# Weight sums by VectorE instead of accumulating DMAs, and w_down loaded one chunk earlier, in a streaming encoder trunk

## The chip, the core and the metric

The kernel runs on one NeuronCore of a Trainium2 chip. The core has a matrix engine (TensorE, PE in the profile), a vector engine (VectorE, DVE), a scalar engine (ScalarE, ACT), GpSimd (POOL) and SyncE (SP), which here only issues DMAs. Every engine works through its own queue in order, and waits at the head of it for the semaphores of what it reads and overwrites. The metric is the device time of one execution in microseconds; the median of several runs is compared.

## The reference

Two layers of an encoder trunk run on 512 prompt frames and 64 sample frames (576 tokens) of width 1024. Each layer has a mixer with three kinds of attention and then a gated feed-forward, which is where the change lies:

```python
x = x + merge_branches(o_a, o_b, o_c, gate_pre, b_gate[l], w_branch[l], w_out[l])
xn = rmsnorm(x, norm_ffn[l])
gu = xn @ w_up                      # (tokens, 1024) @ (1024, 2 * 2816)
g, u = gu[..., :D_FF], gu[..., D_FF:]
c = conv_b + sum_k conv_w[k] * shifted(g, k)     # causal, width 3
h = gelu(c) * u
x = x + h @ w_down                  # (tokens, 2816) @ (2816, 1024)
```

All inputs, weights and outputs are float32.

## The kernel before

The 2816 hidden columns are 22 blocks f of 128. A float32 product is made of three matmuls on rounded operands: every operand is split into a high part (a cast) and a low part (the operand minus its high part), and high times high, high times low and low times high are summed in PSUM. The 576 tokens are two halves of 288, so a matmul has 288 columns.

Blocks 0 to 3 (`ffn_f`) compute gate and up columns directly. Blocks 4 to 21 (`unit_f`) use a Strassen-Winograd scheme on the two-by-two product of (gate, up) columns, each cut into an upper and a lower half of the 1024 rows, with the two token halves. It takes seven products per block instead of eight: A11, P, R, A12, Q, A22, V, in this order, of 4 row tiles times 3 matmuls, so 84 matmuls. The weight operands of the seven are, with G and U for gate and up columns and 1, 2 for upper and lower rows: A11 = G1, A12 = G2, A22 = U2, P = U1 + U2, R = U1 + G1, Q = P + G1, V = Q + G2.

`wforms` prepares the raw operands of every block, one after another. It uses three raw buffers of 512 KB: r1 holds P in its first half and R in its second, r0 holds G1 and G2, and q holds Q and V; a22 (256 KB, U2) is a tile of the general pool of 40 slots. In the kernel before, U1 is loaded twice into r1, once for each half; r0 and a22 are loaded; GpSimd then issues two accumulating DMAs, which add a22 to the first half and G1 to the second; VectorE computes Q and V from them. `wparts` splits a raw operand: ScalarE casts the high part; the low part comes from VectorE, or, for A11, A12 and A22 (`by_dma`), from ScalarE writing minus the high part and GpSimd issuing an accumulating DMA that adds the raw operand (line 1361). `wparts` for a block waits until TensorE has been given the same form of the block before.

The three loads of the next block wait for their buffers: r1 until P and R of this block are split and Q is made, r0 until A11 and A12 are split and R, Q and V are made, a22 until A22 is split.

Between the blocks stand the down products, in chunks of 2 x 128 output columns, one behind each block: with a group of four hidden blocks a chunk has 4 outputs of 12 matmuls, 48 in all (blocks 8 to 20), with a group of two 24 (blocks 4 to 7). Most chunks bring their own weights through `down_own`: two loads of raw w_down (tiles dr), then casts (dh) by ScalarE and low parts (dl) by VectorE. `all_own` runs these one chunk after another.

The order of all queues is written by a planner while the program is built. `charge` advances a clock for each compute engine by an estimated cost; generators (`spawn`, `tick`) emit their next step when the clock of TensorE has come to their own time. `pause(ns)` puts a generator off by so much of the planned TensorE clock, and `until` until a condition on what has been emitted holds. Nothing of this exists at run time: it only fixes where in each queue an instruction stands. Semaphores do the rest. PSUM has five banks of the kind "z"; A11 and A12 share one (ScalarE copies A11 away to `s` before A12 adds to it, line 1473, and copies A12 to `gp` afterwards, lines 1479 and 1481), P and Q share another, and four outputs of a down chunk take one each until VectorE has added them to x. Behind a block, `tail` runs the convolution (`conv_steps`), the GELU product `ge`, and the split of the result into hh and hl.

In the profile's names, wr are the raw weights (r1, r0, q, a22), m0f13A is the product bank of A11 and A12 of block 13 in layer 0, whi...a and wlo...a its weight parts, eh and el the parts of P and R (b) and A22 (d), md a down product. Layer 0 is the 0 behind the first letter, layer 1 the 1.

Of the kernel before, what the change touches and what calls it, by code (L numbers as in the profile page):

```python
# [14 lines left out]
ALU = mybir.AluOpType  # L15

P = 128
D = 1024
# [29 lines left out]
def trunk_kernel(ctx: ExitStack, tc: tile.TileContext, a: dict, o: dict):  # L48
    nc = tc.nc
    dma = nc.sync.dma_start  # L50
# [14 lines left out]
    def slot(nm, dt=F32, w=TOK):  # L65
        return sp_.tile([P, GW], dt, tag="s", name=nm, bufs=NS)[:, 0:w]
# [29 lines left out]
    def charge(eng, cost):  # L96
        start = clk[eng] if cx["eng"] == eng and cx["last"] == cx["t"] else max(clk[eng], cx["t"])
        clk[eng] = start + cost
        cx["t"] = cx["last"] = clk[eng] + 70
        cx["eng"] = eng  # L100
# [39 lines left out]
    vector = Engine(nc.vector, "DVE", dve_cost)  # L140
# [11 lines left out]
    def spawn(label, g, first=False):  # L152
        gens.insert(0 if first else len(gens), [label, g, cx["t"]])
# [30 lines left out]
    def pause(ns):  # L184
        cx["t"] = clk["PE"] + ns
        yield

    def until(cond):
        while not cond():
            cx["t"] = clk["PE"] + 1  # L190
            yield
# [1000 lines left out]
    def layer(l):  # L1192
# [65 lines left out]
        def ffn_f(f):  # L1258
# [27 lines left out]
            def fin():  # L1286
# [8 lines left out]

            chunk(f"g{nm}", a["w_up"][l][:, f * P:(f + 1) * P], ND, act, evg, pre_ev=pre,
                  pre=begin_ffn if f == 0 else (lambda: spawn("wf", wforms())) if f == NORD - 1 else None, norm=[1] if f == 0 else None,
                  post=lambda: (spawn(f"c{l}{f}", conv()), spawn("forms", forms()) if f == 0 else None))

# [56 lines left out]
        def low(out, src, hi, by_dma):  # L1356

            if by_dma:
                scalar.activation(out, hi.bitcast(F32), AF.Copy, scale=-1.0)
                charge("POOL", 900)  # L1360
                nc.gpsimd.dma_start(out, src, accum_op=ALU.add)
            else:
                vector.tensor_tensor(out, src, hi.bitcast(F32), op=ALU.subtract)
# [4 lines left out]
        def half_tile(nm, dt=F32):  # L1368
            return slot(nm, dt)[:, 0:512].rearrange("p (k c) -> p k c", k=4)

        def wparts(f, nm, forms_, src, by_dma, small):

            if f > NORD:
                yield from until(lambda: all((f - 1, n) in used for n in forms_))
            elif nm == "a":
                yield from until(lambda: "last" in fast)
            elif nm in "cd":
                yield from until(lambda: "go" in fast)
            yield
            key = f"{l}{f}{nm}"  # L1380
            if small:
                pairs = [(half_tile(f"eh{key}{j}", F32R), half_tile(f"el{key}{j}", F32R))
                         for j in range(len(forms_))]
            else:
                h_, l_ = (wp.tile([P, 8, P], F32R, tag=t, name=f"{t}{key}", bufs=2) for t in ("whi", "wlo"))
                pairs = [(h_[:, 4 * j:4 * j + 4, :], l_[:, 4 * j:4 * j + 4, :]) for j in range(2)]
            for j, n in enumerate(forms_):
                hi, lo = pairs[j]
                scalar.copy(hi, src[:, 4 * j:4 * j + 4, :])
                yield  # L1390
                low(lo, src[:, 4 * j:4 * j + 4, :], hi, by_dma)
                ws[f, n] = (hi, lo)
                made.add((f, n))
                yield

        def wforms():

            w = a["w_up"][l]
            rr = lambda t: t.rearrange("(k p) c -> p k c", p=P)
            for f in range(NORD, NF):  # L1400
                gc, uc = w[:, f * P:(f + 1) * P], w[:, F + f * P:F + (f + 1) * P]

                def raw(i, *need):
                    if f > NORD:
                        yield from until(lambda: all((f - 1, n) in made for n in need))
                    return wp.tile([P, 8, P], F32, tag="raw", name=f"wr{l}{f}{i}", bufs=3)

                r1 = yield from raw(1, "P", "R")
                for j in range(2):
                    dma(r1[:, 4 * j:4 * j + 4, :], rr(uc[0:D // 2]))  # L1410
                r0 = yield from raw(0, "A11", "A12")
                dma(r0, rr(gc))
                if f > NORD:
                    yield from until(lambda: (f - 1, "A22") in made)
                a22 = half_tile(f"wr{l}{f}3")
                dma(a22, rr(uc[D // 2:D]))
                spawn("wa", wparts(f, "a", ("A11", "A12"), r0, f != NORD + 1, False), True)
                yield from pause(5000)
                for j, t in enumerate((a22, r0[:, 0:4, :])):
                    charge("POOL", 900)  # L1420
                    nc.gpsimd.dma_start(r1[:, 4 * j:4 * j + 4, :], t, accum_op=ALU.add)  # L1421
                spawn("wd", wparts(f, "d", ("A22",), a22, True, True), True)
                yield from pause(4500)
                spawn("wb", wparts(f, "b", ("P", "R"), r1, False, True), True)
                q = yield from raw(2, "Q", "V")
                vector.tensor_tensor(q[:, 0:4, :], r1[:, 0:4, :], r0[:, 0:4, :], op=ALU.add)
                yield
                vector.tensor_tensor(q[:, 4:8, :], q[:, 0:4, :], r0[:, 4:8, :], op=ALU.add)
                yield
                spawn("wc", wparts(f, "c", ("Q", "V"), q, False, False), True)  # L1430

        def down_own(c, fs, d2, after):

            yield from until(after)
            n = len(fs) // 2
            src = down_w(fs, d2).rearrange("(k p) c -> p k c", p=P)
            key = f"{l}{fs[0]}{d2}"
            raw = [slot(f"dr{key}{j}")[:, 0:n * 256].rearrange("p (k c) -> p k c", k=n) for j in range(2)]
            for j in range(2):
                dma(raw[j], src[:, n * j:n * j + n, :])  # L1440
            yield from pause(4000)
            hi, lo = ([slot(f"d{t}{key}{j}", F32R)[:, 0:n * 256].rearrange("p (k c) -> p k c", k=n)
                       for j in range(2)] for t in "hl")
            for j in range(2):
                scalar.copy(hi[j], raw[j])
                yield
                vector.tensor_tensor(lo[j], raw[j], hi[j].bitcast(F32), op=ALU.subtract)
                yield
            c["lo"] = [lo[k // n][:, k % n, :] for k in range(2 * n)]
            c["hi"] = [hi[k // n][:, k % n, :] for k in range(2 * n)]  # L1450
# [108 lines left out]
        def down_w(fs, d2):  # L1559
            return a["w_down"][l][fs[0] * P:(fs[-1] + 1) * P, d2 * 2 * P:(d2 + 1) * 2 * P]  # L1560
# [53 lines left out]
        def all_own():  # L1614
            for n, (c, fs, d2) in enumerate(owns):
                yield from down_own(c, fs, d2, lambda: n == 0 or n - 1 in issued)
# [386 lines left out]
```

## Time and profile before

| | us |
|---|---|
| median of three runs (2237.34 to 2241.85) | 2240.66 |
| the profiled execution | 2234.81 |
| its span, from the first to the last instruction | 2232.7 |
| mean granted TensorE clock over the span | 0.984 |

All durations below come from the profiled execution. The granted clock is 1.00 at 2.4 GHz and 0.5 at 1.2 GHz; a value between is a mean over time. In a row of a timeline, the bracket at the end gives the engine's idle time before the instruction and what ended it. In names of groups, buffer numbers are left out. A busy share of TensorE does not say that it works at its peak, since the ends of pipelined matmuls are modelled; the number of matmuls in a stretch says more.

### The profile page before, as it was taken

What the parts mean: (1) busy time and instruction counts of PE and PEld (TensorE: products, weight loads), DVE (VectorE), ACT (ScalarE), POOL (GpSimd) and SP (SyncE); (2) the same over time, 40 slices, a digit from 0 to 9 for tenths busy, and PEclk for the clock granted to TensorE, in tenths of its full rate; (3) what the DMA queues carried; (4) which work ended last, traced back from release to release, by engine and by line L of the source; (5) the groups of instructions that cost most, each with busy time, mean ns of one, the idle gap of its engine ahead of it and who ended that gap; (6) DMA issues with size and microseconds to landing.
All of it is one profiled execution on the core that took longest, in us unless ns stands there. A gap on an engine that the chain in (4) does not pass through costs nothing.

```text
span 2232.7 us, 40248 instructions
## 1 busy us (share of the span) xinstructions
PE 2128.5 (95%) x15479; PEld 2073.0 (93%) x15479; DVE 1465.1 (66%) x3076; ACT 1230.1 (55%) x2485; POOL 467.4 (21%) x687
## 2 busy tenths in 40 slices
PE   8999999999999899898899999999999999998897
PEld 7999999999999898898899999999999998988897
DVE  7876666776568666455678766677755777646555
ACT  5657776555446555445345677754553455545444
POOL 2111220111213322222110122101103233222221
PEclk9999999999999999999999999999999999999999
DMA  7452222332326887666343222233224277766661
GB/s 214 124 147 71 80 71 77 104 93 78 121 83 134 175 185 155 148 148 142 106 121 103 81 70 72 77 101 100 86 79 124 81 169 167 166 156 140 149 158 58
DMA packets 375657, 263.19 MB, mean 118 GB/s; under 512 B 15600, under 2 KB 344242, under 8 KB 375402
## 3 DMA queue, kind: packets, MB, share of 16 engines
q1 hardware_dynamic: 344906, 204.32, 31.2%
q0 software_dynamic: 30560, 56.31, 14.7%
q8 instruction: 122, 2.00, 0.4%
q14 instruction: 69, 0.57, 0.1%
HBM read 185.98 MB, written 25.83 MB: 95 GB/s over the span
## 4 chain that ended last, share of the span: by engine, by line
PE 71%; DMA 13%; DVE 8%; ACT 3%; issue 3%; POOL 1%; SPq 0%; POOLq 0%; DVEq 0%; ACTq 0%
PE md L146 8%; DMA wr<-in_w_up 6%; PE mo L146 4%; DMA wr<-wr 4%; PE mg1a L146 2%; PE mg0a L146 2%; PE mg1b L146 2%; PE mg0b L146 2%; PE mg1c L146 2%; PE mg0c L146 2%; PE mv1a L146 1%; PE mb1a L146 1%; PE mb0a L146 1%; PE mv1b L146 1%; PE mv0b L146 1%
## 5 line engine op out<-in xcount | busy, mean ns | idle before, releaser
L117 DVE TENSOR_TENSOR wr<-wr,wr 128x512 f32<-128x512 f32 x72 | 49.6, 690 | 185.0 <-DMA wr<-wr 184.2
L1421 POOL DMA_DIRECT2D wr<-wr x72 | 65.2, 1095 | 278.7 <-DMA wr<-in_w_up 274.9
L117 DVE TENSOR_TENSOR x<-md,x 128x288 f32<-128x288 f32 x224 | 97.0, 451 | 33.1 <-PE md L146 32.8
L117 ACT CAST dh<-dr 128x512 fp32r<-128x512 f32 (+1 forms) x72 | 41.5, 577 | 134.4 <-DMA dr<-in_w_down 134.4
L146 PE MATMUL md<-hh1f,dh 128*128 128x288 f32 x256 | 81.6, 319 | 16.0 <-ACT gp1f L117 15.3
L146 PE MATMUL md<-hh0f,dh 128*128 128x288 f32 x256 | 81.4, 318 | 16.1 <-ACT gp0f L117 15.4
L146 PE MATMUL md<-hh1f,dl 128*128 128x288 f32 x256 | 82.4, 322 | 9.6 <-DVE dl L117 8.8
L146 PE MATMUL md<-hh0f,dl 128*128 128x288 f32 x256 | 81.7, 319 | 8.1 <-DVE dl L117 7.7
L146 PE MATMUL md<-hl0f,dh 128*128 128x288 f32 x256 | 80.0, 313 | 0.0
L117 DVE TENSOR_TENSOR dl<-dr,dh 128x512 fp32r<-128x512 f32 (+1 forms) x72 | 45.1, 627 | 53.3 <-ACT dh L117 53.3
L146 PE MATMUL md<-hl1f,dh 128*128 128x288 f32 x256 | 79.8, 312 | 0.0
L146 PE MATMUL mo<-ml,whio 128*128 128x288 f32 x256 | 75.7, 296 | 0.8 <-DVE ml L117 0.8
L146 PE MATMUL mo<-mh,whio 128*128 128x288 f32 x256 | 75.7, 296 | 0.0
L146 PE MATMUL mo<-mh,wloo 128*128 128x288 f32 x256 | 75.5, 295 | 0.0
L146 PEld LDWEIGHTS md<-hh1f,dh 128*128 128x128 f32 x256 | 52.7, 206 | 19.1 <-ACT gp1f L117 18.0
L146 PEld LDWEIGHTS md<-hh0f,dh 128*128 128x128 f32 x256 | 52.6, 205 | 18.8 <-ACT gp0f L117 17.6
L146 PEld LDWEIGHTS md<-hh1f,dl 128*128 128x128 f32 x256 | 52.5, 205 | 14.0 <-DVE dl L117 13.9
L146 PEld LDWEIGHTS md<-hh0f,dl 128*128 128x128 f32 x256 | 52.2, 204 | 12.1 <-DVE dl L117 12.0
L146 PEld LDWEIGHTS md<-hl1f,dh 128*128 128x128 f32 x256 | 52.6, 206 | 0.0
L146 PEld LDWEIGHTS md<-hl0f,dh 128*128 128x128 f32 x256 | 52.4, 205 | 0.0
L146 PEld LDWEIGHTS mo<-ml,whio 128*128 128x128 f32 x256 | 48.2, 188 | 1.2 <-DVE ml L117 1.2
L146 PEld LDWEIGHTS mo<-mh,wloo 128*128 128x128 f32 x256 | 48.2, 188 | 0.0
(2903 smaller groups left out, 9479.6 us busy)
## 6 DMA issues: line engine op xcount, KB each, us to landing
wr<-in_w_up SPq DMA_DIRECT2D x108, 256.0 KB
wr<-in_w_up SPq DMA_DIRECT2D x36, 512.0 KB
wr<-wr POOLq DMA_DIRECT2D x72, 256.0 KB, 4.3
dr<-in_w_down SPq DMA_DIRECT2D x56, 256.0 KB
wro<-in_w_out SPq DMA_DIRECT2D x16, 512.0 KB
xspill<-x SPq DMA_DIRECT2D x16, 288.0 KB
x<-xspill SPq DMA_DIRECT2D x16, 288.0 KB
wrg0a<-in_w_in SPq DMA_DIRECT2D x8, 512.0 KB
```

Source lines behind the costliest of these rows:

```text
L117: return f(*args, **kw)
L146: nc.tensor.matmul(out, lhsT=lhsT, rhs=rhs, start=start, stop=stop, skip_group_check=True)
L1421: nc.gpsimd.dma_start(r1[:, 4 * j:4 * j + 4, :], t, accum_op=ALU.add)
```

## The change

In `wforms`, U1 is loaded once, into the second half of r1. The accumulating DMAs are left out: after a pause of 6 us of planned time VectorE adds a22 to it, into the first half (P), and then G1 in place (R). The three generators that split A11 and A12, P and R, and A22 are started behind these two adds, in another order than before. Q and V follow as they did.

In `down_own`, the raw loads of a chunk are issued as soon as the generator reaches it, which is when the split of the chunk before has been emitted; only then comes a pause of 6 us (4 us before) and the wait until the products of the chunk before have been emitted. The casts follow with no further pause.

```diff
--- before.py
+++ after.py
@@ -1406,22 +1406,21 @@
                     return wp.tile([P, 8, P], F32, tag="raw", name=f"wr{l}{f}{i}", bufs=3)
 
                 r1 = yield from raw(1, "P", "R")
-                for j in range(2):
-                    dma(r1[:, 4 * j:4 * j + 4, :], rr(uc[0:D // 2]))
+                dma(r1[:, 4:8, :], rr(uc[0:D // 2]))
                 r0 = yield from raw(0, "A11", "A12")
                 dma(r0, rr(gc))
                 if f > NORD:
                     yield from until(lambda: (f - 1, "A22") in made)
                 a22 = half_tile(f"wr{l}{f}3")
                 dma(a22, rr(uc[D // 2:D]))
+                yield from pause(6000)
+                vector.tensor_tensor(r1[:, 0:4, :], r1[:, 4:8, :], a22, op=ALU.add)
+                yield
+                vector.tensor_tensor(r1[:, 4:8, :], r1[:, 4:8, :], r0[:, 0:4, :], op=ALU.add)
+                yield
                 spawn("wa", wparts(f, "a", ("A11", "A12"), r0, f != NORD + 1, False), True)
-                yield from pause(5000)
-                for j, t in enumerate((a22, r0[:, 0:4, :])):
-                    charge("POOL", 900)
-                    nc.gpsimd.dma_start(r1[:, 4 * j:4 * j + 4, :], t, accum_op=ALU.add)
+                spawn("wb", wparts(f, "b", ("P", "R"), r1, False, True), True)
                 spawn("wd", wparts(f, "d", ("A22",), a22, True, True), True)
-                yield from pause(4500)
-                spawn("wb", wparts(f, "b", ("P", "R"), r1, False, True), True)
                 q = yield from raw(2, "Q", "V")
                 vector.tensor_tensor(q[:, 0:4, :], r1[:, 0:4, :], r0[:, 0:4, :], op=ALU.add)
                 yield
@@ -1431,14 +1430,15 @@
 
         def down_own(c, fs, d2, after):
 
-            yield from until(after)
             n = len(fs) // 2
             src = down_w(fs, d2).rearrange("(k p) c -> p k c", p=P)
             key = f"{l}{fs[0]}{d2}"
             raw = [slot(f"dr{key}{j}")[:, 0:n * 256].rearrange("p (k c) -> p k c", k=n) for j in range(2)]
             for j in range(2):
                 dma(raw[j], src[:, n * j:n * j + n, :])
-            yield from pause(4000)
+            yield from pause(6000)
+            yield from until(after)
+            yield
             hi, lo = ([slot(f"d{t}{key}{j}", F32R)[:, 0:n * 256].rearrange("p (k c) -> p k c", k=n)
                        for j in range(2)] for t in "hl")
             for j in range(2):
```

## Rows read from the trace of the kernel before

**Rows 1.** The page, busy time of each engine over the span.

```profile
PE 2128.5 (95%) x15479; PEld 2073.0 (93%) x15479; DVE 1465.1 (66%) x3076; ACT 1230.1 (55%) x2485; POOL 467.4 (21%) x687
```

**Rows 2.** The table of stretches, busy time and clock; columns stand above.

```profile
core 0: us, PE busy (x) PEld busy (x) DVE busy (x) ACT busy (x) POOL busy (x), PEclk, DMA share, GB/s
792.70:1062.70 270.00, 245.34 (x1718) 238.34 (x1717) 153.91 (x279) 133.34 (x266) 65.88 (x123) 0.96 0.70 155
1896.70:2167.50 270.80, 245.98 (x1718) 238.57 (x1717) 154.64 (x281) 134.01 (x266) 66.18 (x120) 0.96 0.69 153
726.60:792.70 66.10, 60.26 (x433) 57.61 (x433) 44.79 (x82) 37.21 (x78) 20.50 (x36) 1.00 0.81 178
1829.20:1896.70 67.50, 62.00 (x435) 59.26 (x434) 44.98 (x82) 37.27 (x79) 21.44 (x37) 0.97 0.80 178
535.70:581.70 46.00, 46.00 (x351) 46.00 (x350) 18.09 (x33) 24.16 (x39) 0.00 (x0) 1.00 0.29 87
```

**Rows 3.** The table of waits: us in total, times, longest us.

```profile
POOL wr L1421 <- DMA wr<-in_w_up: 274.9, 27, 12.2
DVE wr L117 <- DMA wr<-wr: 184.2, 28, 10.2
ACT dh L117 <- DMA dr<-in_w_down: 134.4, 26, 7.6
```

**Rows 4.** The timeline of SyncE from 880 to 935: start, duration.

```profile
894.04 0.37 SPq L1412 DMA_DIRECT2D wr<-in_w_up  x1
894.52 0.52 SPq L1416 DMA_DIRECT2D wr<-in_w_up  x1
895.14 0.96 SPq L1440 DMA_DIRECT2D dr<-in_w_down  x2
...
915.08 0.37 SPq L1412 DMA_DIRECT2D wr<-in_w_up  x1
```

**Rows 5.** The timeline of GpSimd from 884 to 930: start, duration.

```profile
899.22 1.75 POOL L1421 DMA_DIRECT2D wr<-wr  x2 [9.92 <-DMA wr<-in_w_up]
...
900.29 0.87 POOL L117 COPY gp0f<-pcol 128x2 f32<-128x2 f32 x1
...
908.86 0.86 POOL L1361 DMA_DIRECT2D wlo014a<-wr  x1 [0.31 <-ACT wlo014a L117]
...
920.87 1.75 POOL L1421 DMA_DIRECT2D wr<-wr  x2 [10.83 <-DMA wr<-in_w_up]
```

**Rows 6.** The timeline of ScalarE from 884 to 930.

```profile
899.93 0.62 ACT L117 CAST dh<-dr 128x512 fp32r<-128x512 f32 x1 [5.30 <-DMA dr<-in_w_down]
...
903.03 0.62 ACT L117 CAST eh014b<-wr 128x512 fp32r<-128x512 f32 x1 [2.48 <-DMA wr<-wr]
...
903.56 0.45 ACT L117 COPY gp0f<-m0f13A 128x224 f32<-128x224 f32 x2
...
907.94 0.63 ACT L117 ACTIVATE wlo014a<-whi014a 128x512 fp32r<-128x512 f32 x1
```

**Rows 7.** The timeline of VectorE from 884 to 930.

```profile
892.27 0.75 DVE L117 TENSOR_TENSOR ge0f<-ge0f,u0f 128x576 f32<-128x576 f32 x1
...
903.03 1.42 DVE L117 TENSOR_TENSOR wr<-wr,wr 128x512 f32<-128x512 f32 x2 [8.52 <-DMA wr<-wr]
```

**Rows 8.** The timeline of TensorE from 900 to 915.

```profile
904.07 0.50 PE L146 MATMUL md<-hh0f,dh 128*128 128x288 f32 x1 [1.91 <-ACT gp0f L117]
```

**Rows 9.** Tile m0f13A: ns min, median, max; first and last start.

```profile
L146 PE MATMUL m0f13A<-fh,whi013a x8: 295/296/297, 890.8 to 896.8; 128*128 128x288 f32 x8
```

**Rows 10.** The page, groups of instructions that write wr: mean ns.

```profile
L117 DVE TENSOR_TENSOR wr<-wr,wr 128x512 f32<-128x512 f32 x72 | 49.6, 690 | 185.0 <-DMA wr<-wr 184.2
L1421 POOL DMA_DIRECT2D wr<-wr x72 | 65.2, 1095 | 278.7 <-DMA wr<-in_w_up 274.9
```

**Rows 11.** The timeline of GpSimd from 785 to 800.

```profile
791.43 1.86 POOL L1361 DMA_DIRECT2D wlo08a<-wr  x1
```

**Rows 12.** The timeline of VectorE from 785 to 800.

```profile
791.73 1.67 DVE L117 SCALAR_TENSOR_TENSOR c0f<-gp0f,pcol,c0f 128x578 f32<-128x578 f32 x2
```


## The prediction

> **What bounds the kernel now.** The page is read first. TensorE is busy for 95% of the span [rows 1], so the kernel seems bound by its matmuls, and only the time that TensorE does not work at its own pace can be won. Where that time lies is read from the table of stretches [rows 2]. Its last row is a stretch of pure matmuls: 351 in 46.00 us, 0.1311 us each, at the full granted clock (1.00, the 2.4 GHz level). The two long stretches of the fast feed-forward (blocks f = 8 to 20, 13 blocks of 84 + 48 = 132 matmuls) hold 1718 matmuls in 270.0 and 270.8 us. At 0.1311 us they would take 225.2, so 44.8 and 45.6 us are lost there: a block takes 20.8 us where its matmuls need 17.3. The early blocks (f = 4 to 7, 108 matmuls each, 14.2 us) lose 66.1 - 56.8 = 9.3 and 67.5 - 56.9 = 10.6 us. Together 110 us; nothing in the change touches matmuls elsewhere. The granted clock of 0.96 in the long stretches, a mean over time at 2.4 and at 1.2 GHz, belongs to this loss.
>
> The table of waits says who is late [rows 3]: GpSimd waits 275 us for w_up loads before it can issue the sums, VectorE 184 us for those accumulating DMAs, ScalarE 134 us for w_down loads. A wait off the path costs nothing, so one block is followed through the queues. SyncE issues the gate columns (r0) at 894.04 and the lower up columns (a22) at 894.52 [rows 4]. GpSimd, which has waited for them, issues the two sums at 899.22 [rows 5]. They land at 903.03, when ScalarE casts the first half of P and VectorE adds Q and V [rows 6, 7]. ScalarE then works in order through copies and casts to the last negation for A12, 907.94 + 0.63 = 908.57 [rows 6]. GpSimd issues its low part at 908.86 [rows 5]; when that has landed the r0 buffer is free, and SyncE issues the next r0 at 915.08 [rows 4]. Its successor's sums are issued at 920.87 [rows 5]. The loop closes:
>
> 3.81 (899.22 to 903.03) + 5.54 (to 908.57) + 0.29 (to 908.86) + 6.22 (to 915.08) + 5.79 (to 920.87) = 21.65 us.
>
> That is longer than the 17.3 us of matmuls: the long stretches are bound by a loop of DMA latencies, and TensorE pays at one place. The two copies that free the first bank (gp0f) stand behind the cast of P in ScalarE's queue, run at 903.56 [rows 6], and the down matmuls start after 1.91 us idle at 904.07 [rows 8].
>
> **The change part by part.** *The sums.* Removed from the loop: 3.81 us, two accumulating DMAs. Added: the P add, of the form and size of the Q and V adds, 0.69 us [rows 10]. R's add runs while ScalarE casts P. On VectorE this makes 72 x 0.69 = 50 us more; in a long stretch 26 x 0.69 = 18 us on 154 of 270 [rows 2], 172 of about 234, 73%, and the engine sits idle 8.52 us just before these adds [rows 7]. GpSimd loses 72 issues of 1.10 us [rows 10] that now only wait. The second load of the common summand (256 KB in a block) goes; it is issued a period ahead of its use, so I count nothing, up to a few tenths of the 5.79 us if its traffic was in the way.
>
> *w_down sooner.* The two loads stand on SyncE's queue just behind a22, at 895.14 [rows 4], and ScalarE waits 5.30 us for them, until 899.93 [rows 6]. The accumulating DMAs cover this now, since P's cast could not start before 903.03 anyway. With them gone P would be ready at 899.22 + 0.69 = 899.91: the old w_down wait would then be the next late thing. In the changed kernel the loads stand in the same place but serve the next chunk, so the wait goes. Their casts move to the front of the block; the one between P's cast and the last negation leaves the 5.54 us, worth 0.53 (the distance from 903.03 to 903.56 of one instruction to the next [rows 6]). Two raw buffers are held one period longer. If SyncE must wait for them, r1 and r0 stand behind it; r0 is not due for some 19 us (895.14 to 915.08), so this is costed at nothing; beyond that cover each us is a us of the loop.
>
> *The wait that is added.* VectorE now waits itself for a22 and r0, at the head of its queue. Behind it stand the rest of P, R, Q, V, the low parts of w_down, and the sums that free the banks of P and R. The block's matmuls begin at 890.8 [rows 9], its loads land 8.4 us later, and the down chunk wants its low part some 11 us after the beginning (84 x 0.1311). Four adds are 2.8 us: 11.2, about even, if the loads stayed where they are. But they come earlier: the cast for A12 may start only when TensorE has passed A12 of the block before, 4 x 12 x 0.1311 = 6.3 us into it. Half a microsecond of copies (0.45), six casts of 0.62 (3.7), 0.3, 6.22 and 5.79 put the landing 22.8 us after that beginning, which at a period of 18 is 4.8 us into the block instead of 8.4.
>
> The new loop is 21.65 - 3.81 + 0.69 - 0.53 = 18.0 us, above the 17.3 of the matmuls and so the period. Long stretches: 13 x 18.0 = 234, a gain of 36.0 and 36.8. The early blocks have a load of r1, the sums and four casts in their loop, nearer to the matmuls already; between nothing and 9.3 + 10.6 I take half, 10. The sum is 83 us. The profiled execution took 2234.81 us (span 2232.7, 2.1 around it), so 2152 on its scale; it is 5.85 under the median of the runs, 2240.66. On the median's scale **2158**.
>
> **A rule of the skill that speaks against it.** GpSimd issues the remaining low parts in 0.86 us in the long stretches [rows 5], but in 1.86 us where VectorE runs its two-input convolution steps at that moment [rows 11, 12]. The Trainium skill, GPSIMD Engine Reference, section Specifications, says that GpSimd's SBUF interface is shared with VectorE and contends with VectorE instructions that have two SBUF inputs. The rows agree, and the new adds are such instructions. By the rule the issues would go back to the longer time, and by the row alone they stay at 0.86; the price is the second rival.
>
> **The rivals.** *Part of the gain (0.18).* The landing does not move up in the block. VectorE is then blocked until 8.4, and the first low part of w_down follows four adds: 8.4 + 5 x 0.69 = 11.9 against 11.0. As a loss of 3.5 us in a block goes with 1.91 idle today, 0.9 idle is 1.7. Period 19.0: 2 x 13 x 1.8 = 47, with 5 early 52: 2189. For it speaks that the w_down loads still share the engines with r0; against it the relation to A12 above.
>
> *GpSimd's issues stretch (0.10).* Two issues that stand in the loop take 1.0 us more: period 20.0, gain 2 x 13 x 0.8 = 21, with 10 early 31: 2210. For it rows 11 and 12; against it that VectorE's adds come at the landing and the issues some 6 us later.
>
> *The wait moves to where TensorE feels it (0.13), slower.* It decides whether the sums stand before or behind the GELU product (ge, 892.27) in VectorE's queue [rows 7]. If before, the product waits for the loads, ScalarE's cast of it waits, behind that the copy of the A11 bank, and A12's matmuls may not begin before that copy. The loop is then landing, sums, product 0.7, cast 0.6, copy 0.4, A12 1.6, copies 0.5, and from there 4.0 + 6.22 + 5.79: 19.8 and the sums, 21.2 with two of them ahead and 22.6 with four. Against 20.8 today that is 26 x 0.4 = 10 to 26 x 1.8 = 47 us slower: 2251 to 2288. Against it: GpSimd's sums now stand just ahead of the buffer set-up of a new block (900.29) [rows 5], the new pause is 1 us longer, and the product is emitted ahead of that beginning. But 1 us is a narrow margin.
>
> *Nothing changes (0.06).* The loads of r0 and the landing of low parts, 12 of 21.65 us, grow by what the sums give back, as the queues move closer together: 2236 to 2245.
>
> **How the numbers follow.** My forecast has 0.53. Its floor is TensorE without a gap, 2241 - 110 = 2130; with the part gain and the stretched issues it reaches to 2230, and 0.81 lies inside; its own range is 2130 to 2185. About 0.2% (4.5 us) is what a measurement of this kernel can tell from no change. Faster: 0.53 + 0.18 + 0.10 = 0.81; same 0.06; slower 0.13.
>
> **What would show it.** Right: no accumulating DMA on r1, 144 such adds on VectorE, the two long stretches near 234 us at a granted clock near 1.00, ScalarE's wait for w_down nearly gone, no idle TensorE behind gp0f, and VectorE's wait for w_up loads down from 8.5 to some 2 to 5 us in a block. Wrong: TensorE idle at A12 or Q behind a ScalarE copy (the sums stand too early in the queue), SyncE waiting long ahead of the w_down loads (no free buffer), low-part issues of 1.8 us in the long stretches, or r0's issue no longer following the low part of A12, which would mean that the loop I summed is not the one that binds.

## The result, and the profile after

| | us |
|---|---|
| median before, in the runs beside the changed kernel | 2240.26 |
| median after, four runs (2206.68 to 2210.94) | 2209.09 |
| ratio, with its 95% interval | 0.9862 [0.9845, 0.9879] |
| profiled execution before, its span | 2234.81, 2232.7 |
| profiled execution after, its span | 2207.59, 2205.7 |

The kernel became 31 us faster, where 83 were forecast. The time is in the upper third of the whole range, 2130 to 2230, and outside the forecast's own 2130 to 2185; the sign is right, the size is not. It falls beside the 2210 of the rival in which GpSimd's issues stretch, by luck, since that mechanism did not come (see the other rivals). The question is where the other 52 us went.

The page after, two lines that answer to [rows 1, 10]: busy time of each engine, and the group of instructions that writes wr.

```profile
PE 2111.8 (96%) x15479; PEld 2069.2 (94%) x15479; DVE 1514.3 (69%) x3148; ACT 1228.5 (56%) x2485; POOL 425.3 (19%) x615
...
L117 DVE TENSOR_TENSOR wr<-wr,wr 128x512 f32<-128x512 f32 x144 | 98.7, 688 | 69.2 <-DMA wr<-in_w_up 68.0
```

The change was made as described: 144 adds in place of 72, 49 us more on VectorE (50 forecast), 72 GpSimd instructions fewer, and the same 15479 matmuls.

The table of waits after, in the columns of [rows 3].

```profile
DVE wr L117 <- DMA wr<-in_w_up: 68.0, 27, 4.9
...
ACT dh L117 <- DMA dr<-in_w_down: 6.0, 2, 3.8
```

ScalarE's 134 us of waiting for w_down are down to 6, and VectorE now waits for w_up itself, 68 us. These rows look as forecast. What they leave open is shown by cutting the feed-forward at the first matmul of block 4, of block 10 and of block 21. First the kernel before, in the table of stretches with the columns of [rows 2]:

```profile
726.60:829.90 103.30, 96.36 (x697) 92.78 (x697) 69.65 (x126) 58.47 (x121) 32.15 (x57) 1.00 0.82 179
829.90:1062.70 232.80, 209.25 (x1454) 203.17 (x1453) 129.04 (x235) 112.08 (x223) 54.23 (x99) 0.95 0.68 151
1829.20:1932.80 103.60, 97.47 (x698) 94.27 (x697) 69.92 (x126) 58.65 (x121) 32.91 (x57) 0.98 0.80 176
1932.80:2167.50 234.70, 210.51 (x1454) 203.57 (x1453) 129.70 (x237) 112.63 (x223) 54.71 (x99) 0.95 0.67 150
```

And the same table of the changed kernel; the two lines behind the "..." are its blocks 4 to 7 alone, as in [rows 2].

```profile
726.20:857.60 131.40, 105.14 (x699) 101.63 (x698) 79.78 (x143) 58.35 (x124) 26.02 (x46) 0.91 0.47 109
857.60:1050.00 192.40, 192.40 (x1454) 192.40 (x1454) 144.17 (x254) 110.97 (x221) 40.27 (x77) 1.00 0.59 142
1816.00:1948.40 132.40, 105.95 (x698) 102.39 (x698) 80.40 (x143) 58.17 (x124) 25.93 (x46) 0.91 0.47 109
1948.40:2140.90 192.50, 192.50 (x1455) 192.50 (x1454) 142.35 (x254) 111.88 (x221) 39.73 (x77) 1.00 0.58 138
...
726.20:810.60 84.40, 66.87 (x435) 64.06 (x433) 50.36 (x90) 34.65 (x76) 13.82 (x27) 0.90 0.43 102
...
1816.00:1898.40 82.40, 65.71 (x433) 62.85 (x432) 50.27 (x89) 34.52 (x76) 13.82 (x27) 0.92 0.44 104
```

Blocks 10 to 20 now run close to TensorE's own pace: 192.4 us for 11 blocks, 17.5 each (17.3 at 0.1311 us a matmul), busy for every microsecond at a clock of 1.00. They gave 40.4 + 42.2 = 82.6 us. Blocks 4 to 9 took 28.1 + 28.8 = 56.9 us of that back: 103 us became 131 and 132, with the same matmuls, the clock at 0.91 (1.00 and 0.98 before) and the DMA share down from 0.82 and 0.80 to 0.47. The difference of these sums is 25.7 us of the 27.0 by which the span is shorter. So the gain did arrive, and most of it was lost again in blocks 4 to 9, of which 4 to 7 were costed at "half" and 8 and 9 with the long stretches.

The timeline of all engines after, around the start of block 7 (matmuls left out but for the ones that waited):

```profile
782.37 1.42 DVE L117 TENSOR_TENSOR wr<-wr,wr 128x512 f32<-128x512 f32 x2 [0.74 <-DMA wr<-in_w_up]
...
785.56 0.62 ACT L117 CAST eh07b<-wr 128x512 fp32r<-128x512 f32 x1
...
786.08 0.62 ACT L117 CAST whi07a<-wr 128x512 fp32r<-128x512 f32 x1
...
788.19 1.08 POOL L1361 DMA_DIRECT2D wlo07a<-wr  x1
...
792.62 0.61 PE L146 MATMUL m0f7A<-fh,wlo07a 128*128 128x288 f32 x1 [5.33 <-DMA wlo07a<-wr]
...
795.42 0.40 ACT L117 COPY s0f<-m0f7A 128x288 f32<-128x288 f32 x1 [6.18 <-PE m0f7A L146]
795.71 0.62 ACT L117 CAST whi07a<-wr 128x512 fp32r<-128x512 f32 x1
...
797.68 0.86 POOL L1361 DMA_DIRECT2D wlo07a<-wr  x1 [8.13 <-ACT wlo07a L117]
...
801.02 0.40 PE L146 MATMUL m0f7A<-fh,wlo07a 128*128 128x288 f32 x1 [1.09 <-DMA wlo07a<-wr]
...
801.10 0.38 SPq L1411 DMA_DIRECT2D wr<-in_w_up  x1
```

A11 is the first product of a block, and its weights are now made last. Its raw operand was there at the latest when the second of the two adds began, at 783.1 (782.37 + 1.42 - 0.69), but the generator that splits it is started only behind the pause and both adds. Its cast comes at 786.08, behind those of A22 and P (785.56), and its low part is issued at 788.19 and lands 4.4 us later, at 792.62, when TensorE has stood still for 5.33 us (5.32 in block 6 and 5.21 in block 8). Then the second half of the same split, for A12, is queued on ScalarE behind the copy of A11's bank (795.42), which is itself late; its low part is issued 9.5 us behind the first, and the next r0 waits for it until 801.10. The kernel before, in the same place:

```profile
771.73 0.62 ACT L117 CAST whi07a<-wr 128x512 fp32r<-128x512 f32 x1 [1.96 <-DMA wr<-in_w_up]
...
773.31 0.86 POOL L1361 DMA_DIRECT2D wlo07a<-wr  x1 [11.06 <-ACT wlo07a L117]
...
774.97 1.86 POOL L1361 DMA_DIRECT2D wlo07a<-wr  x1
```

There ScalarE casts A11 at the moment at which the load lands, and the two low parts are issued 1.7 us apart.

In the late blocks the same order does no harm, because the operand is there a block ahead: block 16's add runs at 945.98, and its first matmul starts at 962.6. The timeline of all engines after, around block 16:

```profile
944.07 0.75 DVE L117 TENSOR_TENSOR ge0f<-ge0f,u0f 128x576 f32<-128x576 f32 x1
944.84 0.88 SPq L1438 DMA_DIRECT2D dr<-in_w_down  x2
...
945.98 0.69 DVE L117 TENSOR_TENSOR wr<-wr,wr 128x512 f32<-128x512 f32 x1 [1.17 <-DMA wr<-in_w_up]
...
955.15 0.86 POOL L1361 DMA_DIRECT2D wlo016a<-wr  x1 [0.70 <-ACT wlo016a L117]
955.69 1.21 POOL L1361 DMA_DIRECT2D el016d<-wr  x1
...
958.59 0.37 SPq L1411 DMA_DIRECT2D wr<-in_w_up  x1
```

The adds stand behind the GELU product (944.07) and wait 1.17 us. A12's low part is issued 0.5 us ahead of A22's, and the next r0 follows 3.44 us behind it, not 6.22 as in [rows 4, 5].

### The profile page after: what moved, and what is told of

It is laid out like the page before. It is cut to its first block, busy times and chain, and to the rows that moved or that the text cites. A ratio compares the mean times of both kernels' runs of the same rounds, so it can differ in the third digit from the quotient of the medians.

```text
span 2205.7 us, 40108 instructions
## 1 busy us (share of the span) xinstructions
PE 2111.8 (96%) x15479; PEld 2069.2 (94%) x15479; DVE 1514.3 (69%) x3148; ACT 1228.5 (56%) x2485; POOL 425.3 (19%) x615
## 4 chain that ended last, share of the span: by engine, by line
PE 83%; DVE 5%; issue 5%; DMA 4%; ACT 2%; POOL 1%; SPq 0%; POOLq 0%; DVEq 0%; ACTq 0%
PE md L146 10%; PE mo L146 4%; PE mg1a L146 2%; PE mg0a L146 2%; PE mg1b L146 2%; PE mg0b L146 2%; PE mg1c L146 2%; PE mg0c L146 2%; PE mv1a L146 1%; PE mb0a L146 1%; PE mb1a L146 1%; PE mv1b L146 1%; PE mv0b L146 1%; PE mv0c L146 1%; PE mv1c L146 1%
## 5 line engine op out<-in xcount | busy, mean ns | idle before, releaser
L117 DVE TENSOR_TENSOR wr<-wr,wr 128x512 f32<-128x512 f32 x144 | 98.7, 688 | 69.2 <-DMA wr<-in_w_up 68.0
L146 PE MATMUL md<-hh0f,dl 128*128 128x288 f32 x256 | 75.6, 295 | 0.5 <-DVE dl L117 0.5
L146 PE MATMUL md<-hh1f,dl 128*128 128x288 f32 x256 | 75.6, 295 | 0.5 <-DVE dl L117 0.5
L146 PE MATMUL md<-hh0f,dh 128*128 128x288 f32 x256 | 75.5, 295 | 0.0
L146 PE MATMUL md<-hh1f,dh 128*128 128x288 f32 x256 | 75.5, 295 | 0.0
L146 PE MATMUL md<-hl0f,dh 128*128 128x288 f32 x256 | 75.5, 295 | 0.0
L146 PEld LDWEIGHTS md<-hh1f,dh 128*128 128x128 f32 x256 | 48.2, 188 | 0.0
L146 PEld LDWEIGHTS md<-hh0f,dh 128*128 128x128 f32 x256 | 48.1, 188 | 0.0
L146 PEld LDWEIGHTS mo<-mh,whio 128*128 128x128 f32 x256 | 48.1, 188 | 0.0
L117 ACT ACTIVATE xhf<-x,pcol 128x576 fp32r<-128x576 f32 x16 | 12.5, 780 | 63.9 <-DVE x L117 63.9
```

The costliest lines, as they stand in the source:

```text
L117: return f(*args, **kw)
L146: nc.tensor.matmul(out, lhsT=lhsT, rhs=rhs, start=start, stop=stop, skip_group_check=True)
```

## The experiments

All eight compute the whole reference. Medians are of four runs each, ratios, with their 95% interval, are against the kernel before in the same series (2242.9 us for the first four, 2241.64 for the others); they are those on record and not quotients of the two medians. "Early" is the time from the first matmul of block 4 to that of block 10, "late" from there to block 21, for layer 0 and layer 1. The two theories at the outset: A, the early blocks lose because the split of A11 and A12 starts too late; B, they lose because VectorE waits for the loads at the head of its queue. C, D and E came with the second series: C, the copy of A11's bank ahead of the second cast closes a circle through TensorE; D, it is the late first half alone; E, the late blocks gained by the order in the queues and not by where the sums are done.

**1. The split of A11 and A12 started as soon as its load is issued** (changed kernel)

```diff
                 dma(a22, rr(uc[D // 2:D]))
+                spawn("wa", wparts(f, "a", ("A11", "A12"), r0, f != NORD + 1, False), True)
                 yield from pause(6000)
...
-                spawn("wa", wparts(f, "a", ("A11", "A12"), r0, f != NORD + 1, False), True)
```

> Edit on the changed kernel: the generator that splits A11 and A12 is started ahead of the pause and the sums, as before the change; all else stays. Theory A (the start of A11's low part behind the sums costs the early blocks): in the changed kernel the blocks 4 to 9 take 131.4 and 132.4 us where they took 103.3 and 103.6 before; with the early start they go back to 103 or less, so 28 to 29 us less in each layer and 57 less in all: about 2152 (2140 to 2165), TensorE no longer idle 5 us at A11. Theory B (VectorE's own wait for the loads, at the head of its queue, costs the early blocks): the sums stand where they stood, so 2200 to 2209. Both: the blocks 10 to 20 stay at 17.5 us each.

Measured 2144.3 us (2143.75 to 2144.93), 0.9567 [0.9548, 0.9587]; early 101.7 and 98.1, late 192.5 and 192.6. Its table of stretches for layer 0, and its timeline in block 7:

```profile
725.90:827.60 101.70, 96.61 (x699) 95.21 (x697) 79.22 (x143) 60.18 (x125) 23.33 (x45) 0.97 0.64 143
```

```profile
770.44 0.62 ACT L117 CAST whi07a<-wr 128x512 fp32r<-128x512 f32 x1 [0.35 <-DMA wr<-in_w_up]
...
772.02 0.86 POOL L1361 DMA_DIRECT2D wlo07a<-wr  x1 [7.77 <-ACT wlo07a L117]
773.19 0.86 POOL L1361 DMA_DIRECT2D wlo07a<-wr  x1 [0.31 <-ACT wlo07a L117]
```

The cast is at the landing again, the low parts are 1.2 us apart, and no matmul of A11 in block 7 waits. The early blocks return to what they were and a little below; the late ones keep their gain. VectorE still does the sums where it did, and this edit does not touch its queue. A is right, and B falls. This is the fastest kernel of all, 98.6 us under the one before in its series.

**2. The sums alone** (changed kernel, with `down_own` of before)

```diff
+            yield from until(after)
             n = len(fs) // 2
...
-            yield from pause(6000)
-            yield from until(after)
-            yield
+            yield from pause(4000)
```

> The changed kernel with the w_down loads of the kernel before (issued after the chunk before has been emitted, pause of 4 us behind them). My loop of the prediction: ScalarE's cast of w_down then waits for its loads about where P is ready, and the loop of a late block is 18.5 instead of 17.5 us: 22 late blocks, about 22 us slower than the changed kernel, 2225 to 2235. Theory that w_down was covered anyway: no difference to the changed kernel, 2205 to 2212.

Measured 2222.66 us, 0.9914 [0.9895, 0.9933], between the two expectations. Late 194.1 and 195.0 (17.6 to 17.7 a block), so the wait for w_down, which is still on ScalarE (84.0 us in its table of waits, 134.4 before [rows 3]), costs a late block 0.2 us; early 134.2 and 135.1, 2.7 to 2.8 us more than with the whole change. The late gain does not need w_down sooner.

**3. w_down sooner alone** (kernel before, with `down_own` of after: the diff of the second hunk of the change)

> The kernel before with only the w_down loads a chunk sooner; sums by accumulating DMAs as before. My loop: the accumulating DMA still holds P's cast until its landing, only one cast (0.5 us) leaves the loop: 0 to 13 us faster than before, 2227 to 2240. Theory that ScalarE's 134 us of waiting for w_down was itself on the path: 30 us or more faster, under 2212.

Measured 2205.4 us, 0.9837 [0.9817, 0.9857]: as fast as the whole change. Early 110.6 and 110.5, late 210.9 and 212.7 (19.2 and 19.3 a block). My expectation fell, and the number of the other theory (under 2212, the wait for w_down on the path) came out. GpSimd and SyncE in its timeline, block 14:

```profile
903.28 1.75 POOL L1421 DMA_DIRECT2D wr<-wr  x2 [6.29 <-DMA wr<-in_w_up]
...
912.34 0.86 POOL L1361 DMA_DIRECT2D wlo014a<-wr  x1 [0.70 <-DMA wr<-in_w_up]
912.88 1.21 POOL L1361 DMA_DIRECT2D el014d<-wr  x1
...
921.71 1.75 POOL L1421 DMA_DIRECT2D wr<-wr  x2 [6.67 <-DMA wr<-in_w_up]
```

```profile
916.22 0.37 SPq L1412 DMA_DIRECT2D wr<-in_w_up  x1
```

And GpSimd in the kernel before, at the place of [rows 5]:

```profile
906.52 0.86 POOL L1361 DMA_DIRECT2D wlo014a<-wr  x1 [5.33 <-DVE dl L117]
907.69 0.86 POOL L1361 DMA_DIRECT2D el014d<-wr  x1 [0.31 <-ACT el014d L117]
```

The accumulating sums are still there, yet the loop is 921.71 - 903.28 = 18.43 us in this block where it was 21.65. From the sums to A12's low part takes 9.06 us (9.64 before), and the r0 load follows 3.88 us behind that, where it took 6.22. The move of two loads changed the order in which the planner writes the queues: A12's low part now stands ahead of A22's (912.34, 912.88), where it was third (908.86 [rows 5], behind 906.52 and 907.69). So the 6.22 us, which my sum kept as a price of the hardware, belonged to one order of the queue. The profile's table of DMA issues has the landings: in the kernel before 3.3, 4.7 and 6.1 us behind the issues at 906.52, 907.69 and 908.86, so each lands some 2.5 us behind the one ahead of it; here, as the second of three, A12's part takes 3.8 us. How much of the 37 us is the order and how much the wait that ScalarE no longer has, this run does not separate; run 8 has the order alone.

**4. The split of A11 and A12 started last of the three, behind the adds** (changed kernel). The planner takes a generator that was started later first, so this puts it in front of the other two; its start stays behind the pause and the adds.

```diff
-                spawn("wa", wparts(f, "a", ("A11", "A12"), r0, f != NORD + 1, False), True)
                 spawn("wb", wparts(f, "b", ("P", "R"), r1, False, True), True)
                 spawn("wd", wparts(f, "d", ("A22",), a22, True, True), True)
+                spawn("wa", wparts(f, "a", ("A11", "A12"), r0, f != NORD + 1, False), True)
```

> The changed kernel with the three splits started at the same late point, but in the order that lets A11 and A12 go first in each round instead of last. Theory A in the form 'the late start': A11's cast is still behind the sums and the convolution; it gains only the one or two casts and the one DMA issue that stood ahead, some 2 us in each of about 10 early blocks: 2185 to 2200. Theory A in the form 'the order among the three': most of the 57 us comes back, 2150 to 2165. Theory B: no change, 2205 to 2212.

Measured 2182.12 us, 0.974 [0.9721, 0.9759]; early 117.1 and 118.4. TensorE in its timeline, block 7:

```profile
784.36 0.61 PE L146 MATMUL m0f7A<-fh,wlo07a 128*128 128x288 f32 x1 [3.90 <-DMA wlo07a<-wr]
```

The wait at A11 shrinks from 5.33 to 3.90 us. The median is 3 us under the range of "the late start" and far from that of "the order among the three". Of the 29.7 and 34.3 us that run 1 wins in the early blocks, the order among the three accounts for 14, and the start itself for the rest.

**5. Both halves of the split written in one step** (changed kernel), so that no copy of A11's bank comes between the casts for A11 and A12.

```diff
                 scalar.copy(hi, src[:, 4 * j:4 * j + 4, :])
-                yield
+                if nm != "a":
+                    yield
                 low(lo, src[:, 4 * j:4 * j + 4, :], hi, by_dma)
...
-                yield
+                if nm != "a" or j:
+                    yield
```

> The changed kernel, but the split of A11 and A12 is emitted in one step (both casts and negations behind one another), still started late. In the changed kernel's early blocks the second cast stands behind ScalarE's copy of the same block's A11, which waits for the low part of A11 to land: a loop of 24 us (load 5.9, to A11's issue 5.8, landing 4.4, A11 and its copy 2.8, cast, negation and issue 2.3, landing 3.4). Theory C (this circle is what makes the early blocks long): without it the loop is about 16, so most of the 57 us comes back: 2155 to 2170. Theory D (the late first half alone, the 5 us that TensorE waits at A11, makes them long): that wait stays in each block, 19 to 20 us a block, 2185 to 2195.

Measured 2186.18 us, 0.9747 [0.9728, 0.9765]; early 118.1 and 120.0. TensorE in its timeline, block 7:

```profile
786.34 0.61 PE L146 MATMUL m0f7A<-fh,wlo07a 128*128 128x288 f32 x1 [3.73 <-DMA wlo07a<-wr]
```

With the copy out of the way the wait for the low part of A11 stays, at 3.73 us. What goes with the copy (C) is 13.3 and 12.4 us in the early blocks, less than half of what run 1 wins there; the late first half (D) keeps the rest, and the median is in D's range. Run 4 also has the cast for A12 ahead of that copy (781.11 against 787.17 in block 7), so its 14 us and these are largely the same gain, and not two to be added.

**6. The low parts of A11 and A12 by VectorE in blocks 5 to 9** (changed kernel), without the accumulating DMA that TensorE waits for.

```diff
-                spawn("wa", wparts(f, "a", ("A11", "A12"), r0, f != NORD + 1, False), True)
+                spawn("wa", wparts(f, "a", ("A11", "A12"), r0, f == NORD or f > NORD + 5, False), True)
```

> The changed kernel, with the low parts of A11 and A12 made by VectorE and not by an accumulating DMA in the blocks 5 to 9. Theory C and D: the landing of 4.4 and of 3.4 us go from the early blocks, which are 15 to 17 us long with 1 to 2 us of waiting at A11 as in block 5 now: 2155 to 2175. Theory B (VectorE's queue is what holds the early blocks): eight adds of 0.69 us more on it in these blocks make them no shorter: 2205 or more.

Measured 2187.63 us, 0.9756 [0.9736, 0.9776]; early 115.6 and 116.0, late 196.7 and 197.1 (the first block whose low part comes by DMA again, block 10, has TensorE waiting 2.49 us for it). It was above what the theory of the late split gave and well under what B gave. TensorE in its timeline, block 7:

```profile
780.67 0.40 PE L146 MATMUL m0f7A<-fh,whi07a 128*128 128x288 f32 x1 [2.73 <-ACT whi07a L117]
...
783.12 0.61 PE L146 MATMUL m0f7A<-fh,wlo07a 128*128 128x288 f32 x1 [1.92 <-DVE wlo07a L117]
```

With the DMA gone TensorE waits first for the cast and then for the subtraction, 4.65 us together. The latency of the DMA is not the cause; that the split begins late is, whoever does it.

**7. Run 1 with `down_own` of before** (the diffs of runs 1 and 2 together)

> The changed kernel with the split of A11 and A12 started early (the fast one, 2144 us) and the w_down loads as in the kernel before. If either edit alone takes the late blocks to TensorE's pace (the sums alone gave 17.6 us a block, with w_down sooner 17.5): 2144 to 2152. If w_down sooner has a worth of its own, as when it was made alone (37 us): 2165 to 2180.

Measured 2155.12 us, 0.9611 [0.9594, 0.9629], between the two expectations; early 101.0 and 100.6, late 192.4 and 199.7. Once the early blocks are right, w_down sooner is worth some 11 us, 7.1 of them in the late blocks of layer 1 and 2.5 in the early ones there; alone (run 3) it was worth 37. The two parts of the change do not add.

**8. Both halves of the split in one step, in the kernel before** (the diff of run 5; all accumulating DMAs, all loads and `down_own` as before)

> The kernel before, all accumulating DMAs and loads kept, but the split of A11 and A12 emitted in one step; by that it stands ahead of P's casts and of A22's split in the queues of ScalarE and GpSimd. Theory E (the accumulating DMAs were in the loop of r0 only because A12's low part stood behind P's cast and A22's part): the loop of 21.65 us loses the 3.81 of the sums, the casts of P (1.1) and the issue of A22's part (1.2), falls under the 17.3 of the matmuls, and the late blocks go to 17.5 to 18 us: 2150 to 2170. Rival (the sums' own latency bounds P, wherever the split of A12 stands): late blocks stay over 20 us, 2220 to 2245.

Measured 2190.22 us, 0.9767 [0.9745, 0.9789]. Late 199.7 and 198.9, 18.1 to 18.2 a block; early 114.9 and 115.9, 12 us longer than before, which puts the median above the expectation. GpSimd in its timeline, block 14:

```profile
903.20 1.75 POOL L1423 DMA_DIRECT2D wr<-wr  x2 [6.27 <-DMA wr<-in_w_up]
...
907.81 0.86 POOL L1361 DMA_DIRECT2D wlo014a<-wr  x1 [0.32 <-ACT wlo014a L117]
...
921.24 1.75 POOL L1423 DMA_DIRECT2D wr<-wr  x2 [7.03 <-DMA wr<-in_w_up]
```

One engine's order alone makes the loop 18.04 us in this block: A12's low part is issued 4.61 us behind the sums, not 9.64, because its cast no longer stands behind P's. The waits of SyncE's queue from 905 to 917 show what its next loads wait for (L1412 is the load pair of r1, L1414 the load of r0):

```profile
SPq L1412 <- DMA wlo014a<-wr: 11.8, 1, 11.8
SPq L1414 <- DVE el014b L117: 2.2, 1, 2.2
```

A12's low part lands 4.0 us behind its issue and lets the r1 load go (911.98); the r0 load follows at 915.14, 7.33 us behind that issue, because it waits for R's low part by VectorE. So the two loads have changed buffers here, and the landing of A12's low part is no longer the last thing that r0 waits for. For the late blocks E holds: against the 82.6 us that the change gave there, the order alone gives 68.9 (33.1 + 35.8), with not one sum moved to VectorE. In the early blocks the price falls on P, whose first low-part matmul waits for VectorE:

```profile
768.54 0.61 PE L146 MATMUL m0f6P<-fh,el06b 128*128 128x288 f32 x1 [2.64 <-DVE el06b L117]
```

| run | median | early, layers 0 and 1 | late, layers 0 and 1 |
|---|---|---|---|
| before | 2240.26 | 103.3, 103.6 | 232.8, 234.7 |
| the change | 2209.09 | 131.4, 132.4 | 192.4, 192.5 |
| 1, split started at the load | 2144.3 | 101.7, 98.1 | 192.5, 192.6 |
| 2, sums alone | 2222.66 | 134.2, 135.1 | 194.1, 195.0 |
| 3, w_down alone | 2205.4 | 110.6, 110.5 | 210.9, 212.7 |
| 4, split started last of the three | 2182.12 | 117.1, 118.4 | 192.4, 193.7 |
| 5, split in one step | 2186.18 | 118.1, 120.0 | 192.5, 192.5 |
| 6, low parts by VectorE | 2187.63 | 115.6, 116.0 | 196.7, 197.1 |
| 7, run 1 with w_down of before | 2155.12 | 101.0, 100.6 | 192.4, 199.7 |
| 8, split in one step, sums by DMA | 2190.22 | 114.9, 115.9 | 199.7, 198.9 |

## Why the prediction was wrong in size

**The step that failed: the early blocks.** "The early blocks have a load of r1, the sums and four casts in their loop, nearer to the matmuls already; between nothing and 9.3 + 10.6 I take half, 10." Blocks 4 to 7 lost 18.3 and 14.9 us, and blocks 8 and 9, which I had counted with the long stretches, 9.8 and 13.9. Both ends of my bound were gains. The diff moves the start of the split of A11 and A12 behind 6 us of pause and two adds; I named that move as part of the change and gave it no cost, in a stretch where the operand lands just ahead of the product that needs it. In the early blocks of before TensorE was nearly fed (in blocks 6 and 7 no wait is above 0.62 us, all at P), so nothing covered a later A11. Runs 1, 4, 5 and 6 show it: with the start moved back the loss is gone, and about half remains if only the order, the copy or the DMA is mended. In numbers: the 10 us of blocks 4 to 7 came out as -33.2, and the 11 us (4 x 2.8) that the long stretches' term held for blocks 8 and 9 as -23.7, together 78 us under the forecast; the late blocks gave 21 more than forecast. That is 57 us less than 83, and 25.7 is what the traces show.

**The late loop: a gain as forecast, and larger.** Forecast 18.0 us a block, measured 17.5, close to TensorE's own pace. Over blocks 10 to 20 my steps give 22 x 2.8 = 62 us; measured were 82.6. Two terms were off. The blocks took 21.2 to 21.3 us before (232.8 and 234.7 over 11), not the mean of 20.8, which blocks 8 and 9 with 18.0 to 18.6 had lowered. And the 6.22 us for the landing of A12's low part was taken as fixed: it is 3.44 after and 3.88 in run 3, where A12's part is no longer third of three in GpSimd's queue. With 3.44 in place of 6.22 my loop is some 15 us, shorter than the matmuls, and they set the period.

**That the latency of the sums had to go: not so.** I took 3.81 us of accumulating DMAs out of the loop. Run 8 leaves them in and still brings the late blocks to 18.1 to 18.2 us. What had to be broken was the chain in the queues, from the sums over P's cast and A12's cast to A12's low part. Run 8 breaks it by order alone; in the changed kernel the DMAs are gone and the order is another as well, and how much each did there was not separated (run 2 has both). That 18.0 came near 17.5 is therefore in part luck.

**w_down: "The accumulating DMAs cover this now".** Run 3 shows that the price drawn from it was wrong: alone the move is worth 37 us. It moves the casts and the order of GpSimd's queue with them, which a reading of one wait could not show. Beside run 1 it is worth 11.

**The added wait: right.** VectorE waits 68 us in all, at most 4.9. The adds stand behind the GELU product (944.07 against 945.98), so the rival in which TensorE feels them did not occur in the late blocks. In the early ones the adds do stand ahead of that product (782.37 against 789.40 in block 7), but so they do in run 1 (772.58 and 779.76), where the loss is gone. The landing came at 0.9 us into the block (945.1, its first matmul, to 945.98), earlier than the 4.8 forecast; SyncE's w_down loads do wait there (944.84, 3.3 us behind the a22 issue at 941.54), and this cover held.

**The other rivals.** GpSimd's issues did not stretch, and I had misread the row that spoke for it. GpSimd in the kernel before, around that row [rows 11], and then an issue that runs beside such convolution steps, with VectorE's row:

```profile
790.36 2.05 POOL L1421 DMA_DIRECT2D wr<-wr  x2
...
2100.80 0.86 POOL L1361 DMA_DIRECT2D wlo118a<-wr  x1 [1.60 <-ACT c1f L117]
...
2100.74 1.67 DVE L117 SCALAR_TENSOR_TENSOR c1f<-gp1f,pcol,c1f 128x578 f32<-128x578 f32 x2
```

The issue of 1.86 us begins at 791.43, 0.98 us before the two issues ahead of it end (792.41), and ends 0.88 us behind them: its length is its place in a run of issues. The issue at 2100.80 follows none and takes 0.86 us although the two-input steps run beside it for all but a few hundredths. The 1.21 us of the late block after (955.69) and the 1.08 of the early one (788.19, behind 787.53 + 0.86) also begin before the issue ahead has ended. The Trainium skill, GPSIMD Engine Reference, section Specifications, says that GpSimd shares its SBUF interface with VectorE and contends with VectorE instructions that have two SBUF inputs; no run here shows that for these issues. "Part of the gain" came nearest in direction, and its mechanism, a landing that doesn't move up, is not what happened. A rival with a late A11 was missing, although the diff shows the moved line.

**What stays open.** How much of the late gain the sums by VectorE and the order each gave in the changed kernel, and how much of run 3's gain is the wait for w_down and how much the order. Run 1's early blocks still stand 7 to 10 us above their matmuls (91.3 at 0.1311 us); in layer 0 block 4 has 7.6 of it (725.9 to 747.7, with three waits of 1.47 to 1.60 us and a granted clock of 0.88), and the rest was not followed.

## What to carry to other kernels

Sum the loop for each stage that an edit runs in, the ramp too, and treat a generator's moved start as a moved latency: ask which product needs its result first and what has been covering it. In a kernel whose queues are written by a planner, a latency read between two rows belongs to the order of the queues; an edit that moves a load can reorder them, so derive the order after the edit before keeping a term. When a part seems to bring the gain, run the other part alone, and an edit that changes only the order: here another order, with the sums left where they were, gave 69 us in the late blocks, where the whole change gave 83.

## What the runs showed of the hardware that I had not expected

This idle stretch cost more than itself. The table of stretches after, for the 5.1 us that follow TensorE's wait of 5.33 us:

```profile
792.60:797.70 5.10, 5.08 (x21) 5.09 (x22) 0.69 (x1) 1.97 (x4) 0.02 (x1) 0.50 0.11 33
```

The granted clock is at 0.50, the 1.2 GHz level, and 21 matmuls take 5.1 us where they need 2.75 at 0.1311 us: 2.3 us behind an idle time of 5.33. In blocks 4 to 9 of before, where no idle time of layer 0 was above 1.1 us, the clock was 1.00 there. So this wait was worth about 7.7 us of block 7, which took 23.8 us (786.8 to 810.6) instead of 14.2. The wait for A12's low part is another 1.09; the last 0.8 is not followed.
